# Adding up a feed-forward layer's output in PSUM: ScalarE puts y into the bank ahead of each row tile

## The chip, the cores and the metric

The kernel runs on one core of a Trainium2 chip. A core has a matrix engine (TensorE, PE in the profile), a vector engine (VectorE, DVE), a scalar engine (ScalarE, ACT), a general one (GpSimd, POOL), and SyncE (SP), whose queue issues most of the loads. Matrix products are summed in PSUM, eight banks that hold 128 x 512 float32 numbers each; all else lies in SBUF, and weights come from memory by DMA. The metric is the time of one execution in microseconds (us), lower being better.

## The reference

One encoder layer on x, 256 rows of 2048 float32 numbers: a feed-forward half step, a mixing step, a second feed-forward half step. Cut to what matters:

```
def _swiglu(x, w_gate, w_up, w_down):
    return (jax.nn.silu(x @ w_gate) * (x @ w_up)) @ w_down

def _macaron_ffn(x, pre_g, w_gate, w_up, w_down, post_g):
    return x + 0.5 * _rms_norm(_swiglu(_rms_norm(x, pre_g), w_gate, w_up, w_down), post_g)

def _gated_mixers(h, ...):          # u = rms_norm(h); projections, Fourier mixing, attention, gates
    return h + _rms_norm(merged @ w_out, post_g)

h = _macaron_ffn(x, ffn1...); h = _gated_mixers(h, ...); return _macaron_ffn(h, ffn2...)
```

_rms_norm(y, g) is y * rsqrt(mean(y * y) + 1e-6) * g, row by row. w_gate and w_up are 2048 x 5632, w_down is 5632 x 2048.

## The kernel before

**Products.** Each float32 product is made of three products of a shorter type (mm3, L107 to L110): every operand is split into a high part (an ACT copy, L103) and a low part (a DVE subtraction, L104). A weight piece is 128 x 1024 numbers. So each piece costs one ACT copy and one DVE subtraction before PE uses it in 12 matmuls.

**Tiles.** The 256 rows are two row tiles, t = 0 and 1. Columns go in blocks of 512. The 5632 inner columns of a feed-forward layer are 11 blocks, f. For each, swiglu makes 256 x 512 gated values, and row_line multiplies them with the block of w_down: 4 column blocks cb by 2 row tiles, each summed over four k slices in a PSUM bank (pr). The results of all 11 blocks have to be added: y, two SBUF tiles of 128 x 2048.

**The line.** Blocks 0 and 1 are made plainly. From then on a Line holds six split weight pieces ahead of PE: feed first lets PE use the oldest piece (next, L511) and then splits a new one; what a caller hands over as `then` is put behind the matmuls of its piece. Inside the line the order on PE, DVE and ACT is exactly the order of the code (tc.manual_schedule, L677). The line alternates row_line of a block, whose gated values are already there, with swiglu of a later one. A layer has 9 swiglu calls in its line, so the kernel has 18.

**A swiglu in the line** makes gate and up products (pc; g0, g1, u0, u1, p1, p5, p6, p7). Five pairs of k slices are done by seven products instead of eight, so the results need additions afterwards: `sums` (an ACT copy L554, DVE additions L550), `gates` (two DVE additions x<-pc,x L550, then the two ACT silus L558), `ups` (DVE L550 and L562). `gates` stands behind the matmuls of the last but one piece, `ups` behind those of the last one. The next matmuls on PE are those of the row block, pr.

**How y is added up before.** row_line's `out` knows three ways: the first block of the line is copied from PSUM to y by ACT (L634); the following eight are copied by ACT to an SBUF tile `part` (L637), and POOL issues a DMA that adds `part` to y (L638); the line's last one is added by DVE (L640).

**The last row block** of each layer, and of the mixing step's w_out, is last_rows. row_part makes a pr tile and DVE adds y to it (L220); PostNorm.block squares y on ACT with a row sum (L371) and multiplies y by the norm's weights on POOL (L372); `sums` and `scale` make the reciprocal root on DVE in small steps (L157 to L168); `add` makes h = h + y*c on DVE (L391). Between layers NextInput.times multiplies h by the next norm's weights (DVE L405), and `turn` transposes it on PE (L178) and splits it, which gives the operand of the next products. There DVE's order is written out by hand (L304 to L341). I call the passage from the first layer to the mixing step the first passage (about 684 to 730 us of the profile), that from w_out to the second layer the second passage (about 1280 to 1322 us), and the end of the second layer, where h is stored, the tail (1980 us on).

PSUM is used as five banks for products (pmm) and three for transposes and some of the seven products (ptr).

Of the kernel before, what the change touches and what calls it, by code (L numbers as in the profile page):

```python
# [10 lines left out]
F32 = mybir.dt.float32  # L11
# [3 lines left out]
AF = mybir.ActivationFunctionType  # L15
ALU = mybir.AluOpType
AX = mybir.AxisListType

P = 128
# [27 lines left out]
B8 = 12  # L47
PLAIN = 2
BY_SEVEN = (0, 1, 2, 4, 6)
Y_BY_DMA = True  # L50
CH = 3
WARM = 8
F_AHEAD = 4
# [4 lines left out]
def encoder_layer(  # L58
# [30 lines left out]
    def work(name, shape=None):  # L89
        return wk.tile(shape or [P, NB], F32, tag="wk", name=name)  # L90
# [13 lines left out]
        v = V.tensor_tensor(out=lo, in0=src, in1=hi.bitcast(F32), op=ALU.subtract)  # L104
        latest["A"], latest["V"] = a.ins, v.ins

    def mm3(ps, lh, ll, rh, rl, first, last):  # L107
        T.matmul(ps, lh, rh, start=first, stop=False)  # L108
        T.matmul(ps, lh, rl, start=False, stop=False)  # L109
        return T.matmul(ps, ll, rh, start=False, stop=last)  # L110

    ident = const.tile([P, P], F32, name="ident")

# [94 lines left out]
                    mm = mm3(ps[t][:], u[t][0][:, kk, :], u[t][1][:, kk, :], *wt[k], kk == 0, kk == KD - 1)  # L208
        return ps

    def row_part(ch, wt, t, cb, y, first=False, part=slice(0, NB)):
        ps = pmm.tile([P, NB], F32, tag="mm", name="pr")[:, part]
        ts = slice(t * P, (t + 1) * P)
        dst = cbs(y[t], cb)[:, part]
        for k in range(CK):
            mm = mm3(ps, ch[0][:, k, ts], ch[1][:, k, ts], *(w[:, part] for w in wt[k]), k == 0, k == CK - 1)
        if first:
            A.activation(dst, ps, AF.Copy)
        else:
            V.tensor_tensor(out=dst, in0=ps, in1=dst, op=ALU.add)  # L220
        return mm
# [32 lines left out]
    def last_rows(ch, w, rb, y, norm, nxt=None, w_next=None):  # L254


        ws = [weights(w[rb, cb], spare=SPARE[cb]) for cb in range(D // NB)]

        def row(t, cb):
            mm = row_part(ch, ws[cb], t, cb, y)  # L260
            norm.block(t, cb)
            return mm

        if nxt is None:
            for t in range(NT):
                for i, (lo, n) in enumerate(norm.parts):
                    cb, part = lo // NB, slice(lo % NB, lo % NB + n)
                    row_part(ch, ws[cb], t, cb, y, part=part)
                    norm.block(t, i)
# [72 lines left out]
        for kg in range(KD // CK):  # L342
            col(1, kg)
        return ps
# [6 lines left out]
    def cbs(a, cb):  # L351
        return a[:, cb * NB:(cb + 1) * NB]

    class PostNorm:
# [10 lines left out]
            lo, n = self.parts[i]  # L365
            return a[:, lo:lo + n]

        def block(self, t, i):
            y = self.part(self.y[t], i)
            junk = work("junk", [P, self.parts[i][1]])  # L370
            A.activation(junk[:], y, AF.Square, accum_out=self.ssq[t][:, i:i + 1])  # L371
            nc.gpsimd.tensor_tensor(out=y, in0=y, in1=self.part(self.g, i), op=ALU.mult)  # L372

        def sums(self, t):
            up = (8.0 / 3.0 / self.half) ** 2
# [142 lines left out]
            while self.queue:  # L518
                self.next()

    def swiglu(line, forms, w, hs):


        ps, begun, x = {}, set(), {}
# [22 lines left out]
        def add(out, a, b):  # L547
            if out not in x:
                x[out] = work(out)
            V.tensor_tensor(out=x[out][:], in0=ps[a][:], in1=x[b][:], op=ALU.add)  # L550
# [5 lines left out]
        def silu(t):  # L556
            g = x["x" + "13"[t]]
            A.activation(g[:], g[:], AF.Silu)  # L558
# [6 lines left out]
        def seven(pair, between=None, *then):  # L565
# [27 lines left out]
            if between:  # L593
# [3 lines left out]

        sums = [copy, lambda: add("x2", "p6", "x1"), lambda: add("x3", "p7", "x2"), lambda: add("x2", "p5", "x2"),
                lambda: add("x5", "p5", "x3")]
        gates = [lambda: add("x1", "g0", "x1"), lambda: add("x3", "g1", "x3"), lambda: silu(0), lambda: silu(1)]  # L600
        ups = [lambda: add("x2", "u0", "x2"), lambda: times(0), lambda: add("x5", "u1", "x5"), lambda: times(1)]
        for kg in range(KD // CK):
            a, b = 2 * kg, 2 * kg + 1
# [8 lines left out]
                seven(a, lambda: plain(b, 0))  # L612
                plain(b, 1)

    def row_line(line, ch, w, rb, y, way, ahead):

        for cb in range(D // NB):
            ps = []

            def use(b, i, cb=cb, ps=ps):  # L620
                if i == 0:
                    if cb in ahead:
                        ahead[cb]()
                    ps.extend(pmm.tile([P, NB], F32, tag="mm", name="pr") for _ in range(NT))
                for t in range(NT):
                    for j in range(WP):
                        k = i * WP + j
                        mm3(ps[t][:], ch[0][:, k, t * P:(t + 1) * P], ch[1][:, k, t * P:(t + 1) * P], *b[j],
                            k == 0, k == CK - 1)

            def out(t, cb=cb, ps=ps):
                dst = cbs(y[t], cb)
                if way == "set":
                    A.activation(dst, ps[t][:], AF.Copy)  # L634
                elif way == "dma":
                    part = work("part")
                    A.activation(part[:], ps[t][:], AF.Copy)  # L637
                    nc.gpsimd.dma_start(dst, part[:], accum_op=ALU.add)  # L638
                else:
                    V.tensor_tensor(out=dst, in0=ps[t][:], in1=dst, op=ALU.add)  # L640

            for i in range(CK // WP):
                line.feed(lambda i=i, cb=cb: ring(raw_piece(w[rb, cb], i)[:]), lambda b, i=i, use=use: use(b, i),
                          *([lambda t=t, out=out: out(t) for t in range(NT)] if i == CK // WP - 1 else []))

    def ffn(u, rs, wg, wu, wgu, wd, yname, tail, gate0, w_next=None, early=()):

# [29 lines left out]
        with tc.manual_schedule(engines={mybir.EngineType.DVE, mybir.EngineType.Activation, mybir.EngineType.PE}):  # L677
            for f in range(PLAIN, nblk + 1):
                if f == 4:
                    norm, nxt = tail(y)  # L680

                def ahead(hs=hs, f=f):
                    chs.append(new_chunk("hT")) if f > PLAIN else None
                    turn_h(chs[-1], hs)

                way = "set" if f == PLAIN else "dma" if Y_BY_DMA and f < nblk else "add"
                before = {D // NB - 1: ahead}
                if f == PLAIN:
                    before[0] = lambda: forms.chunk(KD // CK - 1)
                row_line(line, chs[-1] if f > PLAIN else chs[0], wd, f - 2, y, way, before)  # L690
                if f < nblk:
                    hs = []
                    swiglu(line, forms, wgu[f - PLAIN], hs)
            line.end()
        return last_rows(chs[-1], wd, nblk - 1, y, norm, nxt, w_next), nxt

# [6 lines left out]
    idle = pmm.tile([P, NB], F32, tag="mm", name="idle")  # L703
    for _ in range(WARM):
        T.matmul(idle[:], zero[:, 0:P], zero[:], start=True, stop=True)
    u = [new_u(t) for t in range(NT)]
    h, rs = {}, {}

# [600 lines left out]
```

## Time and profile before

| | |
|---|---|
| time, median of 3 runs | 2018.36 us (2016.18 to 2018.55) |
| profiled execution: its own time | 2016.12 us |
| profiled execution: its span, first to last instruction | 2014.4 us |
| TensorE clock granted, mean | 0.999 |
| DVE, POOL, ACT busy | 86%, 8%, 61% of the span |

The profile shows one execution. A line gives the engine, the line of the kernel (L12), the operation, what it writes and reads (out<-in), the shape, and how often. "mean ns" is the duration of one. Behind a bar stands the engine's idle time just before such instructions, with what ended it ("<-DVE x" means that the wait ended when DVE had written x). Timelines give the start in us, the duration, and the wait in brackets; "x2" there joins two instructions in a row. A matmul of 512 columns is listed with 0.39 us, but they follow each other closer than that, since they overlap: their starts tell the rate.

### The profile page before, as it was taken

What the parts mean: (1) busy time and instruction counts of PE and PEld (TensorE: products, weight loads), DVE (VectorE), ACT (ScalarE), POOL (GpSimd) and SP (SyncE); (2) the same over time, 40 slices, a digit from 0 to 9 for tenths busy, and PEclk for the clock granted to TensorE, in tenths of its full rate; (3) what the DMA queues carried; (4) which work ended last, traced back from release to release, by engine and by line L of the source; (5) the groups of instructions that cost most, each with busy time, mean ns of one, the idle gap of its engine ahead of it and who ended that gap; (6) DMA issues with size and microseconds to landing.
All of it is one profiled execution on the core that took longest, in us unless ns stands there. A gap on an engine that the chain in (4) does not pass through costs nothing.

```text
span 2014.4 us, 26315 instructions
## 1 busy us (share of the span) xinstructions
PE 1993.5 (99%) x9200; PEld 1652.1 (82%) x9200; DVE 1728.4 (86%) x2324; ACT 1231.5 (61%) x1702; POOL 160.9 (8%) x174
## 2 busy tenths in 40 slices
PE   9999999999999999999999999999999999999998
PEld 7888888888888878888888888878888888888886
DVE  6898899988999888887877895878998898988987
ACT  7566666666666556556666554556666666666663
POOL 0001100111101110100000000200011100111002
PEclk9999999999999999999999999999999999999999
DMA  8678877878777696854555557566778877788773
GB/s 325 207 255 229 248 239 225 235 227 246 241 228 229 231 294 194 262 188 142 192 194 184 188 172 278 186 211 198 251 220 237 237 241 235 223 236 239 236 236 115
DMA packets 137173, 451.03 MB, mean 224 GB/s; under 512 B 15016, under 2 KB 21168, under 8 KB 134864
## 3 DMA queue, kind: packets, MB, share of 16 engines
q1 hardware_dynamic: 114256, 411.66, 60.2%
q0 software_dynamic: 22784, 37.69, 11.2%
q8 instruction: 72, 1.18, 0.2%
q14 instruction: 61, 0.50, 0.1%
HBM read 409.44 MB, written 6.29 MB: 206 GB/s over the span
## 4 chain that ended last, share of the span: by engine, by line
PE 93%; DVE 4%; DMA 1%; ACT 1%; issue 1%; SPq 0%; DVEq 0%; ACTq 0%
PE pc L108 19%; PE pc L109 19%; PE pc L110 19%; PE pr L108 10%; PE pr L110 10%; PE pr L109 10%; PE pt L178 1%; DVE wlo L104 1%; DMA raw<-in_w_fo 1%; DVE h L391 1%; PE pe L108 0%; PE pe L109 0%; PE pe L110 0%; PE pt L997 0%; PE pf L110 0%
## 5 line engine op out<-in xcount | busy, mean ns | idle before, releaser
L104 DVE TENSOR_TENSOR wlo<-raw,whi 128x1024 fp32r<-128x1024 f32 (+1 forms) x711 | 858.4, 1219 | 149.7 <-ACT whi L103 142.4
L103 ACT ACTIVATE whi<-raw 128x1024 fp32r<-128x1024 f32 (+1 forms) x711 | 741.2, 1055 | 392.9 <-PE pc L110 117.4
L108 PE MATMUL pc<-whi,fh 128*128 128x512 f32 x1062 | 413.1, 389 | 0.0
L109 PE MATMUL pc<-wlo,fh 128*128 128x512 f32 x1062 | 413.1, 389 | 0.0
L110 PE MATMUL pc<-whi,fl 128*128 128x512 f32 x1062 | 413.1, 389 | 0.0
L108 PE MATMUL pc<-whi,uh 128*128 128x512 f32 x688 | 271.6, 395 | 1.0 <-ACT uh L719 1.0
L110 PE MATMUL pc<-whi,ul 128*128 128x512 f32 x688 | 269.3, 392 | 1.9 <-DVE ul L104 1.9
L109 PE MATMUL pc<-wlo,uh 128*128 128x512 f32 x688 | 269.0, 391 | 2.1 <-DVE wlo L104 2.0
L108 PE MATMUL pr<-whi,hTh 128*128 128x512 f32 x688 | 269.5, 392 | 0.0
L110 PE MATMUL pr<-whi,hTl 128*128 128x512 f32 x688 | 267.8, 389 | 0.0
L109 PE MATMUL pr<-wlo,hTh 128*128 128x512 f32 x688 | 267.8, 389 | 0.0
L110 PEld LDWEIGHTS pc<-whi,fl 128*128 128x128 f32 x1062 | 199.3, 188 | 41.5
L108 PEld LDWEIGHTS pc<-whi,fh 128*128 128x128 f32 x1062 | 199.3, 188 | 41.5
L109 PEld LDWEIGHTS pc<-wlo,fh 128*128 128x128 f32 x1062 | 199.3, 188 | 41.3
L104 DVE TENSOR_TENSOR wlo<-t,whi 128x1024 fp32r<-128x1024 f32 (+1 forms) x180 | 171.5, 953 | 48.0 <-ACT whi L103 48.0
L103 ACT ACTIVATE whi<-t 128x1024 fp32r<-128x1024 f32 (+1 forms) x180 | 152.1, 845 | 93.2 <-DVE t L545 92.9
L545 DVE TENSOR_TENSOR t<-raw 128x512 f32<-128x512 f32 x270 | 178.0, 687 | 3.1
L110 PEld LDWEIGHTS pc<-whi,ul 128*128 128x128 f32 x688 | 129.3, 188 | 29.7 <-DVE ul L104 3.1
L109 PEld LDWEIGHTS pc<-wlo,uh 128*128 128x128 f32 x688 | 129.3, 188 | 28.4 <-DVE wlo L104 3.5
L108 PEld LDWEIGHTS pc<-whi,uh 128*128 128x128 f32 x688 | 129.4, 188 | 27.9 <-ACT uh L719 2.6
L110 PEld LDWEIGHTS pr<-whi,hTl 128*128 128x128 f32 x688 | 129.1, 188 | 26.9
L108 PEld LDWEIGHTS pr<-whi,hTh 128*128 128x128 f32 x688 | 129.2, 188 | 26.4 <-DVE x L550 0.3
(336 smaller groups left out, 2225.5 us busy)
## 6 DMA issues: line engine op xcount, KB each, us to landing
raw<-in_f_gu SPq DMA_DIRECT2D x288, 512.0 KB, 5.2
raw<-in_f_down SPq DMA_DIRECT2D x176, 512.0 KB, 5.2
raw<-in_w_in SPq DMA_DIRECT2D x112, 512.0 KB, 4.7
raw<-in_f_up SPq DMA_DIRECT2D x32, 512.0 KB, 4.5
y<-part POOLq DMA_DIRECT2D x64, 256.0 KB, 6.7
raw<-in_w_ao SPq DMA_DIRECT2D x32, 512.0 KB, 4.3
raw<-in_w_out SPq DMA_DIRECT2D x32, 512.0 KB, 4.2
yf<-part POOLq DMA_DIRECT2D x64, 256.0 KB, 6.2
```

The source lines that it names most:

```text
L103: a = A.activation(hi, src, AF.Copy)
L104: v = V.tensor_tensor(out=lo, in0=src, in1=hi.bitcast(F32), op=ALU.subtract)
L108: T.matmul(ps, lh, rh, start=first, stop=False)
L109: T.matmul(ps, lh, rl, start=False, stop=False)
L110: return T.matmul(ps, ll, rh, start=False, stop=last)
L178: T.transpose(pt[:, j, :], src[:, j * P:(j + 1) * P], ident[:])
L391: V.scalar_tensor_tensor(out=h, in0=self.part(self.y[t], i), scalar=self.c[t][:, 0:1], in1=h, op0=ALU.mult, op1=ALU.add)
L545: V.tensor_tensor(out=out, in0=a, in1=b, op=ALU.subtract)
```

## The change

What DMA, POOL and DVE added outside PSUM is now added in PSUM. ScalarE copies the old y into the bank (a "seed"), the matmuls of the block add to what is there, and ScalarE copies the sum back to y. The new class Rows takes row_line's place: seed(cb) makes the two banks of a column block and seeds them; the seeds of block cb+1 are issued with the first matmuls of block cb; those of the first column block, seed(0), are handed to swiglu, which puts them last in `gates`, behind the two silus. The first row block of the line is not seeded. This removes the 128 copies to `part`, the 128 adding DMAs and the 16 additions of L640; it adds 144 seeds and leaves 144 copies from PSUM to y.

In last_rows each tile is seeded as well, so that the DVE addition L220 goes. The squares read PSUM. The multiplication by the norm weights reads PSUM too: between layers DVE does it instead of POOL, and waits for the square of the same tile; in the tail ACT copies PSUM to y and POOL multiplies as before. The eight warm-up matmuls at the start go over all five product banks.

```
-    def row_part(ch, wt, t, cb, y, first=False, part=slice(0, NB)):
+    def row_part(ch, wt, t, cb, y, first=False, part=slice(0, NB), onto=False):
...
+        if onto:
+            A.activation(ps, dst, AF.Copy)
         for k in range(CK):
-            mm = mm3(ps, ch[0][:, k, ts], ch[1][:, k, ts], *(w[:, part] for w in wt[k]), k == 0, k == CK - 1)
+            mm = mm3(ps, ch[0][:, k, ts], ch[1][:, k, ts], *(w[:, part] for w in wt[k]), not onto and k == 0, k == CK - 1, onto)
+        if onto:
+            return mm, ps
...
-        def block(self, t, i):
+        def block(self, t, i, ps):
...
-            A.activation(junk[:], y, AF.Square, accum_out=self.ssq[t][:, i:i + 1])
-            nc.gpsimd.tensor_tensor(out=y, in0=y, in1=self.part(self.g, i), op=ALU.mult)
+            sq = A.activation(junk[:], ps, AF.Square, accum_out=self.ssq[t][:, i:i + 1])
+            if self.store:
+                A.activation(y, ps, AF.Copy)
+                nc.gpsimd.tensor_tensor(out=y, in0=y, in1=self.part(self.g, i), op=ALU.mult)
+                return
+            m = V.tensor_tensor(out=y, in0=ps, in1=self.part(self.g, i), op=ALU.mult)
+            tc.add_manual_dep(m.ins, sq.ins.name, mybir.DependencyInfo(mybir.DependencyClass.Sync, mybir.DependencyReason.DATA),
+                              reason="one reader of a PSUM bank at a time")
...
-        gates = [lambda: add("x1", "g0", "x1"), lambda: add("x3", "g1", "x3"), lambda: silu(0), lambda: silu(1)]
+        gates = [lambda: add("x1", "g0", "x1"), lambda: add("x3", "g1", "x3"), lambda: silu(0), lambda: silu(1),
+                 seed]
...
+    class Rows:
...
+        def seed(self, cb):
+            if cb == D // NB:
+                return
+            self.ps[cb] = [pmm.tile([P, NB], F32, tag="mm", name="pr") for _ in range(NT)]
+            if not self.first:
+                for t in range(NT):
+                    A.activation(self.ps[cb][t][:], cbs(self.y[t], cb), AF.Copy)
+
+        def feed(self, line, ch, ahead):
+
+            def use(b, cb, i):
+                if i == 0:
+                    if cb in ahead:
+                        ahead[cb]()
+                    self.seed(cb + 1)
...
+            def out(cb):
+                for t in range(NT):
+                    A.activation(cbs(self.y[t], cb), self.ps[cb][t][:], AF.Copy)
...
-                way = "set" if f == PLAIN else "dma" if Y_BY_DMA and f < nblk else "add"
...
+                    rows = Rows(wd, f - 1, y, False)
+                    swiglu(line, forms, wgu[f - PLAIN], hs, lambda rows=rows: rows.seed(0))
```

What stands where on the engines, in the order of the built programs. Line numbers of the changed kernel differ from the earlier ones: its splits are L102 and L103, the ACT copy and the silus of swiglu L566 and L570, the seeds of the line L640, the copies to y L657.

ACT at the end of one swiglu and the start of the row block, before (x are the gate sums, part the tile that the DMA adds):

```order
L554 ACTIVATE x_2019<-pc 128x512
L103 ACTIVATE whi<-raw 128x1024 x2
L558 ACTIVATE x_2019<-x_2019 128x512
L558 ACTIVATE x_2032<-x_2032 128x512
L103 ACTIVATE whi<-raw 128x1024 x3
L637 ACTIVATE part<-pr 128x512 x2
L103 ACTIVATE whi<-raw 128x1024 x2
L637 ACTIVATE part<-pr 128x512 x2
```

The same place in the changed kernel:

```order
L566 ACTIVATE x_2015<-pc 128x512
L102 ACTIVATE whi<-raw 128x1024 x2
L570 ACTIVATE x_2015<-x_2015 128x512
L570 ACTIVATE x_2028<-x_2028 128x512
L640 ACTIVATE pr<-y_934 128x512
L640 ACTIVATE pr<-y_935 128x512
L102 ACTIVATE whi<-raw 128x1024 x2
L640 ACTIVATE pr<-y_934 128x512
L640 ACTIVATE pr<-y_935 128x512
L102 ACTIVATE whi<-raw 128x1024
L657 ACTIVATE y_934<-pr 128x512
L657 ACTIVATE y_935<-pr 128x512
```

The first two seeds (pr<-y) stand straight behind the silus, and the first matmul of the row block, which stood behind nothing of ACT's but the splits of its weights, now needs the first of them. The order of PE's own instructions is the same here.

DVE in the first passage, from the first reciprocal root's last step on, before (y_930 and y_931 are the row tiles, h_1979 the residual of tile 0, gpre the next norm's weights):

```order
L168 SCALAR_TENSOR_TENSOR cr<-cv,cz 128x1
L220 TENSOR_TENSOR y_931<-pr,y_931 128x512
L391 SCALAR_TENSOR_TENSOR h_1979<-y_930,cr,h_1979 128x512
L405 TENSOR_TENSOR y_930<-h_1979,gpre_1985 128x512
L220 TENSOR_TENSOR y_931<-pr,y_931 128x512
L391 SCALAR_TENSOR_TENSOR h_1979<-y_930,cr,h_1979 128x512 x2
```

The same place in the changed kernel (gpost are the norm's weights; L403 and L417 are the former L391 and L405):

```order
L168 SCALAR_TENSOR_TENSOR cr<-cv,cz 128x1
L382 TENSOR_TENSOR y_935<-pr,gpost_1979 128x512
L403 SCALAR_TENSOR_TENSOR h_1975<-y_934,cr,h_1975 128x512
L417 TENSOR_TENSOR y_934<-h_1975,gpre_1981 128x512
L382 TENSOR_TENSOR y_935<-pr,gpost_1979 128x512
L403 SCALAR_TENSOR_TENSOR h_1975<-y_934,cr,h_1975 128x512 x2
```

Each addition L220 is replaced by one multiplication L382 in the same place, while POOL's multiplications (L372) are gone from both passages. Elsewhere in the first passage the scheduler puts small DVE products for the rotary tables (gcq<-rc,gq, L763 before) some instructions earlier, inside the second reciprocal root, and their loads on SP's queue one weight load earlier.

More of the change, by code (lines that the diff above doesn't have):

```diff
@@ L105, in split, with mm3 @@
         latest["A"], latest["V"] = a.ins, v.ins
[L107 to L110, printed above, removed]
+    def mm3(ps, lh, ll, rh, rl, first, last, onto=False):
+        T.matmul(ps, lh, rh, start=first, stop=False, skip_group_check=onto)
+        T.matmul(ps, lh, rl, start=False, stop=False, skip_group_check=onto)
+        return T.matmul(ps, ll, rh, start=False, stop=last, skip_group_check=onto)
     ident = const.tile([P, P], F32, name="ident")
@@ L519, in end, with swiglu @@
                 self.next()
-    def swiglu(line, forms, w, hs):
+    def swiglu(line, forms, w, hs, seed):
         ps, begun, x = {}, set(), {}
@@ L613, in swiglu, with __init__ @@
                 plain(b, 1)
[L615 to L620, printed above, removed]
+    class Rows:
+        def __init__(self, w, rb, y, first):
+            self.w, self.rb, self.y, self.first, self.ps = w, rb, y, first, {}
+        def seed(self, cb):
[7 more added lines that the diff above has]
+            def use(b, cb, i):
                 if i == 0:
@@ L627, in use @@
                         k = i * WP + j
[L628 to L644, printed above, removed]
+                        mm3(self.ps[cb][t][:], ch[0][:, k, t * P:(t + 1) * P], ch[1][:, k, t * P:(t + 1) * P], *b[j],
+                            self.first and k == 0, k == CK - 1, not self.first)
+            def out(cb):
+                for t in range(NT):
+                    A.activation(cbs(self.y[t], cb), self.ps[cb][t][:], AF.Copy)
+            for cb in range(D // NB):
+                for i in range(CK // WP):
+                    line.feed(lambda i=i, cb=cb: ring(raw_piece(self.w[self.rb, cb], i)[:]),
+                              lambda b, i=i, cb=cb: use(b, cb, i), *([lambda cb=cb: out(cb)] if i == CK // WP - 1 else []))
     def ffn(u, rs, wg, wu, wgu, wd, yname, tail, gate0, w_next=None, early=()):
@@ L689, in ffn @@
                     before[0] = lambda: forms.chunk(KD // CK - 1)
-                row_line(line, chs[-1] if f > PLAIN else chs[0], wd, f - 2, y, way, before)
+                if f == PLAIN:
+                    rows = Rows(wd, 0, y, True)
+                    rows.seed(0)
+                rows.feed(line, chs[-1] if f > PLAIN else chs[0], before)
                 if f < nblk:
                     hs = []
-                    swiglu(line, forms, wgu[f - PLAIN], hs)
+                    rows = Rows(wd, f - 1, y, False)
+                    swiglu(line, forms, wgu[f - PLAIN], hs, lambda rows=rows: rows.seed(0))
             line.end()
@@ L702, in encoder_layer @@
     V.memset(zero[:], 0.0)
-    idle = pmm.tile([P, NB], F32, tag="mm", name="idle")
-    for _ in range(WARM):
-        T.matmul(idle[:], zero[:, 0:P], zero[:], start=True, stop=True)
+    idle = [pmm.tile([P, NB], F32, tag="mm", name="idle") for _ in range(5)]
+    for i in range(WARM):
+        T.matmul(idle[i % 5][:], zero[:, 0:P], zero[:], start=True, stop=True)
     u = [new_u(t) for t in range(NT)]
```

10 lines of the change are left out of this document (4 added, 6 removed).

## Prediction

> **What bounds the kernel now.** I read the page's busy shares and its chain of work first, then the table of windows for where PE stands still, then the timeline of one block, to see how close the other engines run to PE where the change puts something new.
>
> ```profile
> span 2014.4 us, 26315 instructions
> PE 1993.5 (99%) x9200; PEld 1652.1 (82%) x9200; DVE 1728.4 (86%) x2324; ACT 1231.5 (61%) x1702; POOL 160.9 (8%) x174
> PE 93%; DVE 4%; DMA 1%; ACT 1%; issue 1%; SPq 0%; DVEq 0%; ACTq 0%
> q0 software_dynamic: 22784, 37.69, 11.2%
> 200.00:250.00 50.00, 50.00 (x226) 41.49 (x225) 44.01 (x53) 31.09 (x38) 6.86 (x8) 1.00 0.83 238
> 700.00:750.00 50.00, 46.53 (x215) 36.57 (x214) 44.44 (x92) 27.30 (x52) 11.59 (x9) 1.00 0.93 289
> 1300.00:1350.00 50.00, 47.72 (x221) 38.28 (x220) 38.26 (x72) 26.59 (x43) 3.00 (x2) 1.00 0.64 221
> 2000.00:2014.40 14.40, 4.72 (x33) 4.20 (x31) 7.62 (x23) 3.08 (x10) 5.17 (x5) 0.83 0.31 114
> ```
>
> PE is the bound: it stands still for 2014.4 - 1993.5 = 20.9 us in all, and 93% of the chain is PE's. Inside the line (window 200 to 250; behind the window's length come the busy times of PE, weight load, DVE, ACT and POOL, then PE's clock) it has no gap at all: 50.00 of 50.00 us. So nothing that the line sheds on DMA, POOL or DVE can shorten it, while whatever makes PE wait there is paid in full. Gains can come only from the passages (3.47 and 2.28 us of idle PE in their windows) and the tail.
>
> **The seed ahead of the row block.** The new wait is at one place of each of the 18 blocks in the line, where PE goes from swiglu's last product to the row block's first. This is the timeline of one, around 221 us:
>
> ```profile
> 212.24 3.95 DVE L104 TENSOR_TENSOR wlo<-raw,whi 128x1024 fp32r<-128x1024 f32 x3 [0.36 <-ACT whi L103]
> 212.51 1.06 ACT L103 ACTIVATE whi<-raw 128x1024 fp32r<-128x1024 f32 x1 [0.30 <-PE pc L110]
> ...
> 218.10 2.01 DVE L550 TENSOR_TENSOR x<-pc,x 128x512 f32<-128x512 f32 x3
> 220.02 1.22 DVE L104 TENSOR_TENSOR wlo<-raw,whi 128x1024 fp32r<-128x1024 f32 x1
> ...
> 220.87 0.39 PE L110 MATMUL pc<-whi,fl 128*128 128x512 f32 x1
> 221.10 0.39 PE L108 MATMUL pr<-whi,hTh 128*128 128x512 f32 x1
> 221.15 1.28 DVE L550 TENSOR_TENSOR x<-pc,x 128x512 f32<-128x512 f32 x2
> 221.87 1.23 ACT L558 ACTIVATE x<-x 128x512 f32<-128x512 f32 x2 [3.61 <-DVE x L550]
> 223.00 2.00 ACT L103 ACTIVATE whi<-raw 128x1024 fp32r<-128x1024 f32 x2
> ```
>
> PE begins the row block (pr) at 221.10, 0.23 after its last product. The gates' DVE additions begin only at 221.15, since DVE is still at three sums and a split, and the silus follow at 221.87. ACT is free for what stands behind them at 223.00, where the profile has a split and the changed order has seed(0). ACT idles 3.61 us ahead of the silus, but in program order the seed can't use that.
>
> The price of a seed is not in this trace: no ACT instruction copies SBUF to PSUM. The nearest rows are the copy the other way and the silus, which go SBUF to SBUF:
>
> ```profile
> L637 ACT ACTIVATE part<-pr 128x512 f32<-128x512 f32 x128 | 76.2, 596 | 56.5 <-PE pr L110 56.5
> ACT x L558 <- DVE x L550: 65.1, 18, 4.3
> 158.33 0.39 PE L108 MATMUL pr<-whi,hTh 128*128 128x512 f32 x1
> 158.84 1.23 ACT L558 ACTIVATE x<-x 128x512 f32<-128x512 f32 x2 [3.80 <-DVE x L550]
> 159.98 1.99 ACT L103 ACTIVATE whi<-raw 128x1024 fp32r<-128x1024 f32 x2
> 1959.82 0.39 PE L108 MATMUL pr<-whi,hTh 128*128 128x512 f32 x1
> 1960.37 1.23 ACT L558 ACTIVATE x<-x 128x512 f32<-128x512 f32 x2 [3.13 <-DVE x L550]
> 1961.50 1.04 ACT L103 ACTIVATE whi<-raw 128x1024 fp32r<-128x1024 f32 x1
> 711.74 0.50 PE L110 MATMUL pc<-whi,ul 128*128 128x512 f32 x1 [1.14 <-DVE ul L104]
> ```
>
> Two silus take 1.23, so one costs 0.60 to 0.63; the copy costs 0.596. I take 0.60, with 0.5 to 0.7 as bounds. In the block shown the first seed ends at 223.00 + 0.60 = 223.60, 2.50 after PE wanted it. In the first block of the line it is 159.98 + 0.60 - 158.33 = 2.25, in the last 1961.50 + 0.60 - 1959.82 = 2.28. The waits row counts the same wait of the silus 18 times, so every block has it; the same subtraction over all 18 gives 2.2 to 2.6, once 3.1, and 2.4 on average. PE then needs about 0.1 to see that ACT is done, and loses 0.1 because the first matmul after a wait is longer (the last row, from the first passage: 0.50 against 0.39). That is 2.6 us a block, 18 x 2.6 = 46.8 us; with 2.35 and 3.0 as ends, 42 to 54.
>
> It does not wear off. At 212.24 and 212.51 DVE waits for ACT, and ACT for PE: neither has a backlog there, because splits can run only six pieces ahead of PE. The lateness arises anew in the 9 us before each row block, and a PE that was held up by 2.6 us holds up the splits with it.
>
> **The other seeds, and the rest of the line.** The second seed of the pair ends 0.6 after the first, while PE has six matmuls of the first tile (1.36 us at 0.227 each): hidden. seed(1) needs a bank which DVE frees with its next addition; walking the order with the durations above, both are in place about 2.5 us before PE, now itself 2.6 later, gets there; seeds 2 and 3 likewise. Behind the seeds on ACT stand splits of pieces that PE needs several pieces of 2.72 us later. So these cost nothing as long as ACT keeps up: it gains 144 x 0.6 = 86 us, from 61% to some 64% of a longer span. The 128 copies to `part` only change their target. The adding DMAs (queue q0, with 11.2% of the DMA engines' time) and the 16 DVE additions of L640 gave PE no wait, so their going brings nothing. The warm-up over five banks has the same eight matmuls: nothing.
>
> **The passages.**
>
> ```profile
> 703.09 1.56 POOL L372 TENSOR_TENSOR y<-y,gpost 128x512 f32<-128x512 f32 x1 [0.80 <-ACT junk L371]
> 703.42 1.78 DVE L405 TENSOR_TENSOR y<-h,gpre 128x512 f32<-128x512 f32 x1
> L405 DVE TENSOR_TENSOR y<-h,gpre x8: 679/684/1777, 700.4 to 727.4; 128x512 f32<-128x512 f32 x8
> 718.28 0.50 PE L109 MATMUL pc<-wlo,uh 128*128 128x512 f32 x1 [1.02 <-DVE wlo L104]
> 719.13 0.29 DVE L763 TENSOR_TENSOR gcq<-rc,gq 128x128 f32<-128x128 f32 x1 [0.24 <-DMA rc<-in_rope_cos]
> 1311.77 0.50 PE L109 MATMUL pc<-wlo,uh 128*128 128x512 f32 x1 [1.02 <-DVE wlo L104]
> ```
>
> Here PE waits for DVE (1.14 us in the row quoted already, 1.02 twice more), and DVE is slowed by POOL: the L405 that runs beside POOL's multiplication takes 1.78 us, the usual one 0.68. The excess over the shortest of their kind, summed over DVE's instructions that overlap POOL's, is 3.9 us in the first passage and 3.0 in the second. POOL's multiplications leave both, so that excess goes. [...]
>
> Against it stands that DVE's L382 waits for the square, which takes 0.62 and some 0.1 to be seen, where the addition could start at PE's end: 0.7 at each of row tile 1's four tiles if DVE is always there first, 2.8 in all; I count one, since DVE mostly comes late. The gcq products that move into the second reciprocal root cost one more 0.29 there; their table loads move ahead by one weight load as well, and a late table would show as a DVE wait for rc like the 0.24 above. First passage: 3.9 - 0.7 - 0.3 = 2.9 gained, bounds 0.8 and 3.9 (PE's idle time in that window, 3.47, and 0.1 for each of four restarts). Second: 3.0 - 0.7 = 2.3, of which I take 2.0 because PE loses only 2.3 there; bounds 0.2 and 2.6. The eight seeds of each passage have ACT and free banks several tiles ahead: nothing.
>
> **The tail.**
>
> ```profile
> 2004.44 0.28 PE L110 MATMUL pr<-wh,hTl 128*128 128x256 f32 x1
> 2004.76 0.42 DVE L220 TENSOR_TENSOR yf<-pr,yf 128x256 f32<-128x256 f32 x1
> 2005.28 0.42 ACT L371 ACTIVATE junk<-yf 128x256 f32<-128x256 f32 x1 [0.93 <-DVE yf L220]
> 2007.92 0.75 DVE L391 SCALAR_TENSOR_TENSOR h<-yf,cr,h 128x512 f32<-128x512 f32 x1
> 2008.00:2009.00 1.00, 0.00 (x0) 0.00 (x0) 1.00 (x2) 0.00 (x0) 0.00 (x0) 1.00 0.00 0
> 2009.00:2010.00 1.00, 0.00 (x0) 0.00 (x0) 1.00 (x3) 0.00 (x0) 0.00 (x0) 0.81 0.45 176
> ```
>
> The last square no longer waits for DVE's addition: it can start about 2004.8 instead of 2005.28, and all behind it moves by 0.5. ACT's extra copy (about 0.4) and POOL's product end near 2006.7, covered by the reciprocal root, which lasts to 2007.92; without that cover they would cost some 1 us. Bounds 0 and 0.5.
>
> **The sum**, on the profiled execution of 2016.12: + 46.8 - 2.9 - 2.0 - 0.5 = 2057.5 us. The median of the runs, 2018.36, is 2.24 above that execution, so I predict 2060 us, 2.1% slower. A measurement of this kernel can tell about 0.2% from no change. This forecast's own range is 2016.12 + 42 - 7.0 + 2.2 = 2053 to 2016.12 + 54 - 1.0 + 2.2 = 2071; chance 0.75.
>
> **Rivals.**
>
> *The clock falls in each stall* (0.05). In the last two window rows PE's granted clock is still 1.00 between 2008 and 2009, over 3.3 us after the last matmul ended (2004.44 + 0.28), and falls to half only about 2009.6 (0.81 over the last row), after 4.9 us. A stall of 2.6 is well short of that. If it did fall, and rose again only after as long at half rate, each stall would cost 2.4 more, 18 x 2.4 = 43: about 2103 us. [...]
>
> *More of ACT's work comes late* (0.11): seed(1) or the splits behind it. DVE's 86% and the seeds' place ahead of the splits speak for it, the 2.5 us of room against it. At 1 us more a block: + 18, 2078 us.
>
> *The seeds are hidden, and it is faster* (0.07). If the gates come earlier against PE, the seed costs nothing and the gains stay: 2018.36 - 5.4 = 2013 us. It decides at a stall of 5.4 / 18 = 0.3 us a block, so the silus would have to end 2.3 us sooner. For it: ACT idles 3.61 us ahead of them, and DVE has slack over a whole block (44.01 of 50). Against it: the DVE order ahead of the gates (three sums and a split, 218.10 to 221.15) is unchanged and starts without a backlog.
>
> *About nothing* (0.02): a stall near 0.3 us.
>
> The range for 8 in 10 reaches past the first forecast's own to 2080, which takes in the second rival, and down to 2046, where a stall of 2.2 us with the full gains, 2016.12 + 39.6 - 7.0 + 2.2 = 2051, wears off by another eighth because DVE comes less late behind a stalled PE. Left out are the clock, the hidden seeds and the stall of 0.3, 0.14 in all. Faster 0.07, within 0.2% 0.02, slower 0.75 + 0.11 + 0.05 = 0.91.
>
> **What would show it.** Right: in each block of the line the first pr matmul waits 2.3 to 2.8 us for ACT's pr of L640, 18 times, some 45 us in the waits; the window 200 to 250 has PE at about 48 instead of 50.00; the L417 products are all near 0.68 and PE's waits in the passages sum to under 2 us; the clock stays 1.00. Wrong: no such wait (third rival), the clock under 1.00 in such windows (first), waits at the later pr tiles or for whi and wlo in the line (second), or DVE waits for rc or for the square in the passages.

## The result, and the profile after

| | median | range |
|---|---|---|
| before | 2017.55 us | 2016.18 to 2018.55, 4 runs |
| changed | 2073.07 us | 2069.25 to 2077.92, 4 runs |

The ratio is 1.0277, with a 95% interval of 1.0250 to 1.0304: 2.8% slower, where 2.1% was forecast. The profiled execution of the changed kernel took 2069.25 us, the shortest of the four. The mean clock granted to PE was 0.993 in the two shorter of the changed kernel's runs and 0.991 in the two longer ones.

The head of its page (span, busy shares, chain by engine):

```profile
span 2067.5 us, 26007 instructions
PE 2007.7 (97%) x9200; PEld 1659.1 (80%) x9200; DVE 1711.6 (83%) x2298; ACT 1329.6 (64%) x1898; POOL 28.6 (1%) x30
PE 80%; DVE 10%; DMA 3%; issue 3%; ACT 3%; SPq 0%; ACTq 0%; DVEq 0%
```

The span is 53.1 us longer than before. PE's idle time grew by 38.9 us, from 20.9 to 2067.5 - 2007.7 = 59.8. But PE's busy time grew too, by 14.2 us, with the same 9200 matmuls: they ran slower. Of that second part the forecast's sum has only the longer first matmul of each block, some 2 us.

PE's waits, longest first (total us, times, longest):

```profile
PE pr L108 <- ACT pr L640: 40.8, 18, 2.9
PE pc L109 <- DVE wlo L103: 4.0, 3, 3.4
```

The new wait is there, once in each of the 18 blocks. The timeline of the block that the prediction went through:

```profile
223.47 1.28 DVE L562 TENSOR_TENSOR x<-pc,x 128x512 f32<-128x512 f32 x2
224.19 1.23 ACT L570 ACTIVATE x<-x 128x512 f32<-128x512 f32 x2 [3.79 <-DVE x L562]
225.33 1.10 ACT L640 ACTIVATE pr<-y 128x512 f32<-128x512 f32 x2
225.96 0.50 PE L108 MATMUL pr<-whi,hTh 128*128 128x512 f32 x1 [2.12 <-ACT pr L640]
226.30 0.39 PE L109 MATMUL pr<-wlo,hTh 128*128 128x512 f32 x1
```

ACT waits for DVE's gate sums, runs two silus, then the seeds, and PE resumes at the end of the first seed. A seed lasts 0.59 us, and the second starts 0.55 behind the first: the price taken, 0.60, was right.

The windows that answer to those of before (length; busy PE, weight load, DVE, ACT, POOL; clock):

```profile
200.00:250.00 50.00, 47.88 (x216) 39.41 (x215) 42.26 (x50) 34.23 (x46) 0.00 (x0) 1.00 0.60 202
250.00:300.00 50.00, 47.88 (x205) 39.08 (x204) 44.65 (x51) 32.06 (x38) 0.00 (x0) 0.97 0.62 207
700.00:750.00 50.00, 46.60 (x209) 38.28 (x208) 37.88 (x70) 33.17 (x65) 4.55 (x4) 0.93 0.77 240
1300.00:1350.00 50.00, 49.58 (x232) 40.10 (x232) 44.05 (x94) 33.57 (x63) 0.00 (x0) 1.00 0.56 189
```

In the first two rows PE is idle for the same 2.12 us. In the second it does 205 matmuls instead of 216, and the clock column says 0.97. The row is a mean; what happens inside it shows closer up. The last product and the first matmul of that block, on the timeline:

```profile
288.64 0.39 PE L110 MATMUL pc<-whi,fl 128*128 128x512 f32 x1
291.15 0.50 PE L108 MATMUL pr<-whi,hTh 128*128 128x512 f32 x1 [2.12 <-ACT pr L640]
```

The same kernel in windows of 1 us from there (the clock is the third number from the end):

```profile
291.00:292.00 1.00, 0.85 (x4) 0.72 (x5) 0.00 (x0) 1.00 (x3) 0.00 (x0) 1.00 0.89 360
292.00:293.00 1.00, 1.00 (x5) 0.81 (x4) 0.37 (x1) 1.00 (x2) 0.00 (x0) 0.70 0.24 98
293.00:294.00 1.00, 1.00 (x4) 0.80 (x3) 1.00 (x2) 1.00 (x2) 0.00 (x0) 0.50 0.00 0
294.00:295.00 1.00, 1.00 (x4) 0.71 (x4) 0.97 (x2) 0.54 (x2) 0.00 (x0) 0.50 0.29 37
295.00:296.00 1.00, 1.00 (x4) 0.81 (x3) 0.96 (x3) 0.40 (x2) 0.00 (x0) 0.60 0.80 217
296.00:297.00 1.00, 1.00 (x6) 0.78 (x6) 1.00 (x2) 0.77 (x1) 0.00 (x0) 1.00 0.67 270
```

PE starts again at 291.15 at full clock; at 292.4 the clock halves, and at 295.8 it is back: 3.4 us, in which eight matmuls follow each other in 0.43 us instead of 0.227. That costs 1.6 us. It happens behind 5 of the 18 stalls, and not behind the one at 225.96, which is just as long.

The third window holds the first passage, and there the clock fell too. Its timeline on DVE, SP's queue and PE:

```profile
734.11 1.29 SPq L83 DMA_DIRECT2D rc<-in_rope_cos  x1
...
739.74 0.16 DVE L165 TENSOR_TENSOR cu<-cz 128x1 f32<-128x1 f32 x1
742.56 0.29 DVE L784 TENSOR_TENSOR gcq<-rc,gq 128x128 f32<-128x128 f32 x1 [2.66 <-DMA rc<-in_rope_cos]
742.77 0.15 DVE L166 SCALAR_TENSOR_TENSOR cv<-cu,ca 128x1 f32<-128x1 f32 x1
...
744.38 0.80 PE L109 MATMUL pc<-wlo,uh 128*128 128x512 f32 x1 [3.40 <-DVE wlo L103]
```

DVE comes to the rotary product gcq in the middle of the second reciprocal root, and its table, asked for at 734.11, lands only some 8.4 us later. (Before, it was asked for at 713.54, and DVE waited 0.24 us for it at 719.13.) DVE stands for 2.66 us, and the split wlo that PE needs stands behind it. PE waits 3.40 us, more than it ever did there before.

The products by the next norm's weights, with POOL's multiplications gone, are as forecast:

```profile
L417 DVE TENSOR_TENSOR y<-h,gpre x8: 682/684/692, 726.2 to 754.3; 128x512 f32<-128x512 f32 x8
L417 DVE TENSOR_TENSOR yo<-h,gpre x8: 681/691/693, 1320.4 to 1344.0; 128x512 f32<-128x512 f32 x8
```

The longest is 0.693 us now; before it was 1.777, in the product that ran beside POOL's multiplication of 1.56 us. Without such a multiplication beside it none is longer than the rest.

### The profile page after: what moved, and what is told of

It reads as the page before. It is cut to its first block, busy times and chain, and to the rows that moved or that the text cites. A ratio compares the mean times of both kernels' runs of the same rounds, so it can differ in the third digit from the quotient of the medians.

```text
span 2067.5 us, 26007 instructions
## 1 busy us (share of the span) xinstructions
PE 2007.7 (97%) x9200; PEld 1659.1 (80%) x9200; DVE 1711.6 (83%) x2298; ACT 1329.6 (64%) x1898; POOL 28.6 (1%) x30
## 4 chain that ended last, share of the span: by engine, by line
PE 80%; DVE 10%; DMA 3%; issue 3%; ACT 3%; SPq 0%; ACTq 0%; DVEq 0%
PE pc L109 14%; PE pc L110 14%; PE pc L108 14%; PE pr L108 11%; PE pr L110 11%; PE pr L109 11%; DVE wlo L103 6%; DVE x L562 2%; PE pt L178 2%; ACT whi L102 1%; DMA raw<-in_f_down 1%; DVE t L557 1%; DMA raw<-in_f_gu 1%; ACT x L570 1%; DMA raw<-in_w_fo 1%
## 5 line engine op out<-in xcount | busy, mean ns | idle before, releaser
L103 DVE TENSOR_TENSOR wlo<-raw,whi 128x1024 fp32r<-128x1024 f32 (+1 forms) x711 | 859.1, 1219 | 189.3 <-ACT whi L102 183.0
L102 ACT ACTIVATE whi<-raw 128x1024 fp32r<-128x1024 f32 (+1 forms) x711 | 742.2, 1055 | 341.0 <-PE pc L110 118.8
L108 PE MATMUL pr<-whi,hTh 128*128 128x512 f32 x688 | 274.8, 399 | 40.8 <-ACT pr L640 40.8
L103 DVE TENSOR_TENSOR wlo<-t,whi 128x1024 fp32r<-128x1024 f32 (+1 forms) x180 | 171.7, 954 | 68.4 <-ACT whi L102 68.4
L102 ACT ACTIVATE whi<-t 128x1024 fp32r<-128x1024 f32 (+1 forms) x180 | 152.0, 844 | 93.7 <-DVE t L557 93.6
L109 PEld LDWEIGHTS pr<-wlo,hTh 128*128 128x128 f32 x688 | 131.3, 191 | 26.5
```

The costliest lines, as they stand in the source:

```text
L102: a = A.activation(hi, src, AF.Copy)
L108: T.matmul(ps, lh, rh, start=first, stop=False, skip_group_check=onto)
L109: T.matmul(ps, lh, rl, start=False, stop=False, skip_group_check=onto)
```

## The experiments

After the result I held theory A: the loss is the place of seed(0) behind the silus (18 stalls, and a clock that some of them halve), and what the passages should have gained is lost to a late constant. The clock rule in it: PE's clock is halved for one window of 3.41 us after a window in which PE stood still for more than about 1.9 us, with windows that run free of the kernel. I had it from the profile above: a grid with a pitch of 3.413 us can be laid over the trace so that the stalls with a fall behind them have 2.06 us or more inside one cell, and all the others 1.77 or less. I took pitch and phase of that grid as fitted, so runs with other stall lengths had to test it.

**early: the first seeds ahead of the silus.**

```
-        gates = [..., lambda: silu(0), lambda: silu(1), seed]
+        gates = [..., seed, lambda: silu(0), lambda: silu(1)]
```

> The changed kernel with the seeds of the first column block put between the gates' additions and the silus, nothing else. Theory A (the loss is the seeds' place behind the silus, 18 stalls of 2.3 to 3.0 us, 43.7 us in all, 2.5 for slower restarts and 8 for the clock that five of the stalls halve): these 54 us go, PE waits for ACT's pr at most 0.3 us a block, and the time is 2073 - 54 = 2019 us, between 2016 and 2023. Rival (the stall comes from the bank that the seed needs, which DVE's gate addition frees): the second seed still waits for DVE, PE stalls 1 us or more a block, 2036 us or more.

Measured: 2016.35 us, ratio to before 0.9996 (0.9987 to 1.0006). The time is back at that of the kernel before. In its table of waits one is left for a seed, 0.7 us long, instead of 18:

```profile
PE pc L109 <- DVE wlo L103: 3.5, 3, 2.9
PE pr L108 <- ACT pr L639: 0.7, 1, 0.7
```

So the loss was the place of the first seeds in ACT's order. The rival falls: the banks were free in time. The seeds are not quite free even here: followed matmul by matmul against the kernel before, PE loses 0.7 us in the first layer's line and 1.8 in the second's, mostly in steps of about 0.1 us at the first matmul of the second row tile and in the wait of 0.7. The second passage gains 2.1, so that the total hides it.

**mid: the first seeds between the two silus.**

```
-                 lambda: silu(0), lambda: silu(1), seed]
+                 lambda: silu(0), seed, lambda: silu(1)]
```

> The changed kernel with the seeds of the first column block between the two silus. The stall is one silu shorter, 1.7 us instead of 2.3. Theory A (PE's clock is halved for one window of 3.41 us after a window in which PE stood still for more than about 1.9 us, the windows running free): no stall of 1.7 reaches that, the clock stays 1.00 in the line, and the time is 2073 - 18 x 0.6 - 8 = 2054 us. Rival (any stall halves the clock in about 5 of 18 cases): 2062 us and a clock below 1.00 in four to six blocks.

Measured: 2051.99 us, ratio 1.0172 (1.0157 to 1.0187).

```profile
PE pr L108 <- ACT pr L639: 29.4, 18, 2.1
```

The waits fall from 40.8 to 29.4 us, 0.63 a block, which is one silu. Of the 18 stalls, 16 were 1.68 to 1.93 us long, and none of these halved the clock. Two were longer: the one of 2.21 us, ahead of 1669.4, halved it, the one of 2.22, ahead of 1736.2, did not. Each stands alone in its window here:

```profile
1650.00:1700.00 50.00, 47.96 (x209) 39.28 (x208) 40.29 (x49) 33.43 (x44) 0.00 (x0) 0.97 0.55 182
1700.00:1750.00 50.00, 47.95 (x212) 39.39 (x211) 45.53 (x52) 33.84 (x42) 0.00 (x0) 1.00 0.67 225
```

"The clock stays 1.00" missed that one fall, but the time came out as theory A has it, 10 us below the rival.

**late: two useless ACT copies ahead of the first seeds.**

```
-                 lambda: silu(0), lambda: silu(1), seed]
+                 lambda: silu(0), lambda: silu(1), idle_copies, seed]
...
+        def idle_copies():
+            for _ in range(2):
+                A.activation(work("nil")[:], x["x1"][:], AF.Copy)
```

> The changed kernel with two useless ACT copies of a 128x512 SBUF tile between the silus and the seeds, so that each stall is 1.2 us longer, about 3.5. Theory A (more than about 1.9 us of standstill inside one free-running window of 3.41 us halves the clock for the next window): 15 to 18 of the 18 stalls halve the clock, 1.6 us each; 2073 + 18 x 1.2 + 11 x 1.6 = 2112 us. Rival 1 (the clock falls only after a window that is idle throughout): a stall of 3.5 covers one in 3 of 100 cases, so the clock falls in none or one, 2073 - 8 + 21.6 = 2087. Rival 2 (a stall halves the clock in 5 of 18 cases whatever its length): 2095.

Measured: 2107.32 us, ratio 1.0444 (1.0427 to 1.0462).

```profile
PE pr L108 <- ACT pr L643: 59.9, 18, 4.1
```

The stalls were 3.3 to 4.3 us long, and 15 of the 18 halved the clock. Counted over the three kernels, a stall being the time from 0.227 us behind the start of the last product to the start of the first pr matmul:

| kernel | stall at the first seed | stalls with the clock halved behind them |
|---|---|---|
| mid | 1.68 to 1.93 us | 0 of 16 |
| mid | 2.21, 2.22 us | 1 of 2 |
| changed kernel | 2.28 to 3.05 us | 5 of 18 |
| late | 3.31 to 4.27 us | 15 of 18 |

A whole idle window (rival 1) and a fixed share (rival 2) are both excluded by the last row. The time is 5 us below the 2112 of theory A. Of those 5 us, 2.6 are the stalls: they grew by 19.0 us in all, not by 21.6.

The traces' own records of the granted clock give the windows without a fit. In late the clock is halved 18 times (15 stalls, one in the first passage, one in the mixing step, one at the end), and each time it begins a whole multiple of 3.413 us behind the first, up to 1935 us later; in the changed kernel its seven do the same (77, 132, 369, 446, 504 and 518 windows behind the first, which is at 292.394). Cut the stalls at these times, taking a window to end where the clock falls, and look at the longest piece of each stall in one window. The clock was halved behind all 20 stalls with a piece of 1.97 us or more, and behind none of the 32 with 1.85 or less; the other two are 1.91 (late, halved) and 1.93 (mid, not halved). So free-running windows explain why one stall of 2.28 us counts and the next doesn't, and the limit lies near 1.9 us. It holds for the 512-column matmuls of the line: in the mixing step, where matmuls are smaller, the clock fell in four runs behind windows with only 1.0 to 1.5 us of standstill (in late at 951.0), and what else counts there stays open.

**ends_only: the change in the last row blocks alone**, in the kernel before, whose line adds up y by DMA.

```
 # row_part, the first part of last_rows, PostNorm.block, warm-up: as in the change
 # row_line with `part`, the adding DMA and L640: as before
```

> The kernel before with only the second half of the change: seeds in the last row blocks, squares and norm weights from PSUM; the line adds up y by DMA as before. Theory A (what the passages gain is lost again because DVE waits for the rotary table rc inside the second reciprocal root, 2.7 us, and PE's clock falls behind that): DVE waits 2 to 4 us for rc near 716 us, the second passage gains 2 us, the tail 0.5; 2015 to 2018 us, no difference from before. Rival (the wait for rc belongs to the changed line, which sheds its DMAs and shifts the passage): no such wait, and 2017.5 - 5.4 = 2012 us.

Measured: 2015.47 us, ratio 0.9989 (0.9980 to 0.9998). DVE's longest wait in the first passage, and PE's behind it:

```profile
DVE gcq L776 <- DMA rc<-in_rope_cos: 3.3, 1, 3.3
PE pc L110 <- DVE wlo L104: 4.1, 3, 3.5
```

The wait for rc belongs to the change in the last row blocks, not to the line. 2015.47 and the 2016.35 of early are the same within their intervals, so these two times can't tell what seeding in the line, in the right place, is worth.

**The constants.** The next three kernels move only DVE's products for the rotary tables (gcq and its like) behind the last split of the passage, in early, in ends_only and in the kernel before:

```
-            V.tensor_tensor(out=gc[:, t, :], in0=rc[:, t, :], in1=g[:], op=ALU.mult)
+            with tc.issue_after(latest["V"]):
+                V.tensor_tensor(out=gc[:, t, :], in0=rc[:, t, :], in1=g[:], op=ALU.mult)
```

> The changed kernel with the first seeds ahead of the silus, and with DVE's products for the rotary tables put behind the hand-ordered part of the first passage. Theory A (the wait for rc inside the second reciprocal root costs the first passage a PE stall of 3.05 us and the halved clock behind it, 1.6 to 2): the stall falls below 1 us and the clock stays 1.00, so 4 us go from 2016.35: 2012 us, faster than before by 0.2 to 0.3%. Rival (DVE's multiplications L382, which wait for the squares, 3.1 us there, set the passage anyway): PE waits as long for another split of the passage, 2016 us.

> The kernel before with the change in the last row blocks alone, y added up in the line by DMA, and the products for the rotary tables behind the hand-ordered part. Theory A: the PE stall of 3.66 us goes as in the run with the early seeds, about 5 us from 2015.47: 2011 us. It also tells what the seeding in the line is worth by itself: theory A says nothing, so that this one and the one with early seeds differ by less than 2 us. Rival: the line without its 128 adding DMAs is faster by more than that.

> The kernel before with nothing changed but the products for the rotary tables behind the hand-ordered part of the first passage. Theory A (before, DVE waited for rc only 0.24 us, and the products beside it cost another 1 us of DVE, on which PE waits there): 0 to 1.5 us faster, 2016 to 2017.5 us, no difference that can be told. Rival (the products and loads are what makes the whole first passage late): 3 us or more faster, and then the gain of the run with early seeds is not the change's.

Measured: 2017.44 (ratio 1.0004, 0.9995 to 1.0013), 2015.65 (0.9990, 0.9981 to 0.9999) and 2018.98 us (1.0012, 1.0003 to 1.0020). None got what I expected, and the kernel before even lost 0.1%. The timeline of early_rope says why:

```profile
716.16 0.74 DVE L403 SCALAR_TENSOR_TENSOR h<-y,cr,h 128x512 f32<-128x512 f32 x1
720.18 0.43 DVE L103 TENSOR_TENSOR dps<-draw,dps 128x258 fp32r<-128x258 f32 x1 [3.27 <-ACT dps L102]
720.52 0.68 DVE L417 TENSOR_TENSOR y<-h,gpre 128x512 f32<-128x512 f32 x1
...
721.35 1.09 PE L178 MATMUL pt<-ident,y 128*128 128x128 f32 x4 [3.39 <-DVE y L417]
```

With gcq out of the way the scheduler put the next constant into the gap, the low part of the Fourier table dps. Its load was issued at 711.35 and ACT could split it only at 719.73. DVE waits 3.27 us for that, and PE 3.39. The wait had only changed its name. In ends_rope DVE waits 4.4 us for the same split, in before_rope 1.5.

**The other constants as well**: splits and copies of dps, dcs, odd, first, alt and mid behind the passage, on ACT and DVE.

```
+    def split_late(hi, lo, src):
+        with tc.issue_after(behind["A"]), tc.issue_after(behind["V"]):
+            split(hi, lo, src)
...
+    behind = dict(latest)
...
-    split(dps[:, 0, :], dps[:, 1, :], constant(dft_pos, WE + WO)[:])
+    split_late(dps[:, 0, :], dps[:, 1, :], constant(dft_pos, WE + WO)[:])
```

> As the run with the early seeds and the rotary products moved, and the splits and copies of the Fourier constants (dps, dcs, odd, first, alt, mid) are put behind the hand-ordered part of the first passage too, on ACT and DVE. Theory A (the first passage loses to whatever constant stands in DVE's order before its load has landed, some 8 us after issue: moving rc only let the split of dps take its place, with 3.3 us): PE's stall of 3.56 us near 718 us goes, no wait there over 1 us, the clock stays 1.00; 4 to 5 us less than 2017.4, so 2012.5 us, 0.2 to 0.3% faster than before. Rival (PE waits for y of L417 because DVE has too much to do there): the wait stays over 2 us, and the time at 2016 to 2017.

> The kernel before with the change in the last row blocks alone, rotary products and Fourier constants behind the hand-ordered part. Theory A: PE's stall of 4.67 us there goes, 2015.65 - 5 = 2010.5 us. Rival: as for the run with early seeds, 2014 to 2016 us.

> The kernel before with nothing changed but the place of rotary products and Fourier constants. Theory A: without the constants, the passage keeps PE's waits that come from POOL's slowing of DVE (1.14 and 1.02 us and shorter ones), 2 us less than with the rotary products alone moved: 2016 to 2017 us, no difference from before, and 3 to 5 us more than the two runs beside it. Rival (the constants were the whole loss): 2013 us, the same as those.

Measured: 2012.95 (ratio 0.9979, 0.9970 to 0.9988), 2011.41 (0.9971, 0.9959 to 0.9982) and 2015.72 us (0.9991, 0.9982 to 1.0000). All three are within 1 us of what theory A gave. The first two are faster than the kernel before, by 0.2 and 0.3%. The windows around the two passages, first of early_const, then of the kernel before, then of before_const:

```profile
690.00:740.00 50.00, 49.11 (x230) 39.72 (x229) 42.00 (x100) 29.62 (x61) 6.71 (x6) 1.00 0.88 283
1270.00:1320.00 50.00, 49.59 (x232) 40.15 (x231) 43.88 (x91) 32.98 (x63) 0.00 (x0) 1.00 0.55 191
```

```profile
690.00:740.00 50.00, 46.53 (x215) 36.60 (x214) 45.41 (x102) 27.65 (x57) 16.66 (x13) 1.00 0.82 258
1270.00:1320.00 50.00, 47.72 (x222) 38.42 (x221) 43.92 (x72) 27.15 (x50) 11.35 (x8) 1.00 0.52 179
```

```profile
690.00:740.00 50.00, 47.28 (x218) 37.10 (x217) 44.50 (x97) 26.57 (x58) 17.75 (x14) 1.00 0.85 259
1270.00:1320.00 50.00, 47.70 (x221) 38.19 (x219) 44.01 (x73) 27.78 (x52) 11.38 (x8) 1.00 0.51 177
```

PE's idle time in the first passage falls from 3.47 to 0.89 us, in the second from 2.28 to 0.41. Moving the constants alone (before_const) gives 0.75 and nothing. So, by difference, some 1.8 of the 2.6 us in the first passage belong to the change in the last row blocks, as do all 1.9 of the second. That it is POOL's going rather than the rest of that change is argued from the L417 rows (0.693 us at most, where L405 of before_const still has one of 1.784), not tested by itself. ends_const, which keeps the DMA line, is the fastest kernel run here. Its lead over early_const, 0.08%, is within the intervals, but ends_only and ends_rope lead their partners with early seeds as well, by 0.9 and 1.8 us, and the traces agree: against the kernel before, the lines of the two layers together cost 2.5, 2.3 and 2.6 us in early, early_rope and early_const, and 0.7, 0.1 and 0.0 in ends_only, ends_rope and ends_const. Seeding in the line is a small loss even in the right place.

## Why the prediction was right, and where it was off

The direction and the main cause were right: the stall at seed(0) makes up 46 of the 53 us. That the time also fell into the range of 2046 to 2080 us is luck in part. The forecast's own range ended at 2071, below the 2073.07 measured; the stretch up to 2080 was added for late work on ACT, which did not come, and the clock, which did fall, had been left out of it.

By its own steps, on the profiled executions (where a stretch is said to gain or lose, the starts of the same matmuls, which are the same 9200 in the same order but for the place of 18 in the passages, are compared with the kernel before):

- **The stall at seed(0), 46.8 us:** right. The 18 stalls sum to 43.7 us (40.8 of waits, and 0.16 each because the last product is listed with 0.39 us where its like follow each other in 0.227), and the slower restarts add 0.14 each, 2.5: 46.2. With five halved clocks at 1.6 that makes 54.2, and 54.2 is what the two lines lose. That it is made anew in every block was right too. early shows that the place is the cause.
- **The clock stays 1.00:** this step failed. The prediction put the clock's cost at nothing, because in the tail it fell only 4.9 us after the last matmul, and kept the other case as an all-or-nothing rival at 0.05. It fell behind 5 of 18 stalls at 1.6 us each, 8 us. The tail row was read as a delay behind the last matmul. It is as well explained by a window's end: a window from 2006.2 to 2009.6 is idle throughout, and the one before it holds only 1.5 us of standstill. In the line, how much of a stall lay in one window decided, not its length alone: behind pieces of 1.97 us or more the clock was halved 20 times of 20, behind 1.85 or less never in 32. The recorded halvings keep a pitch of 3.413 us, and a window need not be idle throughout: in mid a stall of 2.21 us was enough, with 2.10 of it in one window.
- **The first passage, 2.9 gained:** wrong in sign. POOL's slowing of DVE went, as forecast, and the experiments get 2.6 us less idle time there. But the gcq products moved forward were priced at 0.3 us, with a late table only named as a possible sign. It was late: DVE waited 2.66 us, PE lost 3.56 in one gap, and the clock, halved from 742.95 on for two windows, took about another 2.4. Against what PE had lost there before, that makes 1.2 us lost instead of 2.9 gained: the same matmul that started at 697.90 before and 723.52 after, 25.6 later, is followed by one at 744.79 and 771.58, 26.8 later. The wait for the square, counted with 0.7 us in each passage, was longer on DVE, 2.9 us in the first and 3.4 in the second, but it cost PE little: early_const has the same 2.9 and only 0.89 us of idle PE there.
- **The second passage, 2.0 gained:** right. Idle PE fell from 2.28 to 0.42 us in its window, and the matmuls behind it are 2.1 us less late.
- **The tail, 0.5 gained:** about 0.1. In these rows of the changed kernel

```profile
2057.63 0.28 PE L110 MATMUL pr<-wh,hTl 128*128 128x256 f32 x1
2057.95 0.38 ACT L377 ACTIVATE junk<-pr 128x256 f32<-128x256 f32 x1 [0.69 <-PE pr L110]
2059.03 0.49 DVE L161 TENSOR_TENSOR ct<-cy 128x1 f32<-128x1 f32 x1
2060.80 1.41 DVE L403 SCALAR_TENSOR_TENSOR h<-yf,cr,h 128x512 f32<-128x512 f32 x2
```

  the square does start 0.32 us behind the last matmul's start instead of 0.84, but a step of the root that took 0.25 took 0.49, beside POOL's last product, and 2060.80 is 3.17 behind that matmul where it was 3.48; at the span's end, 9.87 against 9.96 us, 0.1 is left.
- **The other seeds, ACT's load, the DMAs that went: nothing:** right here. PE waits for no other seed, and the stalls and falls account for all that the lines lose. The small waits for second seeds in early show only where the stall is gone.

The sum with the measured terms is 46.2 + 8 + 1.2 - 2.1 - 0.1 = 53.2 us, against 53.1 us of span. The forecast of 41 was short by the clock (8) and the first passage (4.1).

## What to carry to other kernels

Where an engine works in the order of the code, as ACT does in this line, a copy that another engine will wait for belongs ahead of the instructions that wait for somebody else: with the first two of each block's eight seeds behind two silus the kernel lost 2.8%, and with these two ahead of them the whole seeding of the lines cost some 2 us. Where PE is the bound, price a stall of 2 us and more with its chance of a halved clock (here 5 of 18 stalls of 2.28 to 3.05 us, at 1.6 us each), and ask of each small instruction that a scheduler is free to move when its load lands (here the rotary table, 8.4 us after its issue); if one such wait is taken away, look what moves into its place before judging the idea.

## What the runs showed of the hardware

Between the matmuls of the line, PE's granted clock was halved for one window of 3.413 us (once in late for two, behind a stall that ran on into the next) when PE had stood still for about 1.9 us or more of the window before: 0 of 16 stalls of 1.68 to 1.93 us did it, 1 of 2 of 2.21 and 2.22, 5 of 18 of 2.28 to 3.05, 15 of 18 of 3.31 to 4.27. The windows ran on at one pitch through the whole execution (in the changed kernel seven halvings from 292.394 to 2060.497, whole multiples of 3.413 us apart), and where a stall lay in them decided. In the changed kernel PE ran at full clock for 1.1 to 1.4 us first, so the slow matmuls don't stand straight behind the stall and are easily missed among the waits; they show as busy time that grew with the same number of matmuls. The rotary table, 128 KB, landed some 5.5 us after its issue before and 8.4 us after it in the changed kernel, where it was issued 2.3 us behind a store of 1024 KB on the same queue instead of 5.9 us behind it. The store and the load, before, then the store of the changed kernel (its load is shown above):

```profile
707.69 0.33 SPq L84 DMA_DIRECT2D h_spill<-h  x1
713.54 0.33 SPq L84 DMA_DIRECT2D rc<-in_rope_cos  x1
731.86 0.33 SPq L83 DMA_DIRECT2D h_spill<-h  x1
```

Counted from the store, the table landed some 11.4 us later before and 10.7 in the changed kernel: asking earlier for a small load brought it hardly any sooner. That the store held it up is likely by this, but no run moved the store.
